# Hyena input weights: the low halves of a float32 split, by accumulating transfers instead of a GpSimd subtraction

## The chip, the cores and the metric

The kernel runs on one core of one Trainium2 chip. The metric is the device time of one execution in microseconds (us), the median over several runs. The engines of a core are TensorE (PE, with PEld for its weight loads), VectorE (DVE), ScalarE (ACT), GpSimd (POOL) and SyncE (SP), which work side by side and wait for each other by semaphores; a DMA is issued from the queue of SP, ACT or POOL and runs beside them.

## The reference, cut to what matters

The program is two small transformer blocks one after the other; the change lies in the last mixer, a Hyena layer over 512 tokens and 1024 channels:

```python
def hyena_mixer(h, w_in, conv_w, conv_b, f_w1, f_b1, f_w2, f_b2, f_w3, f_b3, freq, skip, w_out):
    L = h.shape[1]
    p = h @ w_in
    u = short_conv(p[..., :(HY_ORDER + 1) * HY_WIDTH], conv_w, conv_b)
    gate = p[..., (HY_ORDER + 1) * HY_WIDTH:]
    parts = jnp.split(u, HY_ORDER + 1, axis=-1)
    k_f = hyena_filters(L, f_w1, f_b1, f_w2, f_b2, f_w3, f_b3, freq)
    z = parts[0]
    for o in range(HY_ORDER):
        z = parts[o + 1] * long_conv(z, k_f[:, o], skip[o])
    return (z * jax.nn.silu(gate)) @ w_out
```

`h @ w_in` is a product of 512x1024 by 1024x4096, all in float32. `long_conv` is a convolution by Fourier transforms.

## The kernel before, in words

**The split product.** Each float32 operand is cut into a high part, rounded to the type float32r, and a low part that holds what the rounding lost. A block of the product is three float32r matmuls for each of 8 slices of the inner dimension: high by high, high by low of the data, and low of the weights by high (`mm3`, L192 to L194). The low part of a weight is `raw - high`.

**The weights.** `weight` prepares a tile of 1024x256 weights in two halves of 128 partitions by 1024 elements (512 KB). For each half SP issues the load into `wraw` (L177), ScalarE copies it to `wh` with rounding (L152, from `split`), and the subtraction `wl = wraw - wh` (L140) goes to the engine that the caller names. The tags `wraw`, `wh` and `wl` have two buffers each: two halves of raw weights, two whole tiles of high and of low parts. So a raw half is loaded again when the subtraction of the half before in its buffer has ended, and the next tile but one can be begun when TensorE has read the last of a tile's high part.

**The Hyena stage.** `hyena` takes 16 such tiles, in the order parts 0 and 1 for four channel groups, then parts 3 and 2; each tile serves two blocks of 128 channels (`block`), 48 matmuls in all, 24 to a block. Behind a block ScalarE and VectorE make the short convolution `v` out of the PSUM bank (L152, then two instructions of L143). Between blocks the generator `step` moves two `chain`s on, each of which takes a group of 128 channels through transposes, `spectrum` (matmuls, a ScalarE copy `spb`, VectorE sums `spt` and `X`), the product with the filter's spectrum `K` (`Y`, `pm`; one of the four products is GpSimd's), VectorE sums `spt` and `X` again, and the inverse transform (L1810, `obank`). `K` is loaded by a DMA from ScalarE's queue (L1782). A scheduler lays down one order of instructions for each engine before the run, and each engine keeps to its order: an instruction that waits holds up all behind it.

The low parts of these 16 tiles are made by GpSimd (`eng=nc.gpsimd`, L1888). GpSimd's other work in the stage is one `pm` product for each long convolution and the gate products `zt`.

Of the kernel before, what the change touches and what calls it, by code (L numbers as in the profile page):

```python
# [9 lines left out]
F32 = mybir.dt.float32  # L10
# [3 lines left out]
AF = mybir.ActivationFunctionType  # L14
ALU = mybir.AluOpType
# [3 lines left out]
P = 128  # L19
S = 512  # L20
D = 1024
# [29 lines left out]
class Kern:  # L51
# [117 lines left out]
    def weight(self, src, kb, gain=None, eng=None):  # L169
        hi, lo = self.hl(self.wp, "w", 2, [P, 8, self.wcols])  # L170
        src = src.rearrange("(k p) c -> p k c", p=P)
        cols = src.shape[-1]
        h = (kb + 1) // 2
        for s in (slice(0, h), slice(h, kb)):
            n = s.stop - s.start
            raw = self.t([P, 4, self.wcols], F32, "wraw", 2, self.wp)[:, :n, :cols]
            self.nc.sync.dma_start(raw, src[:, s, :])  # L177
            hs, ls = hi[:, s, :cols], lo[:, s, :cols]
            if gain is None:
                self.split(raw, hs, ls, eng)  # L180
            else:
                for k in range(n):
                    g = gain[:, s.start + k : s.start + k + 1]
                    self.act(hs[:, k], raw[:, k], AF.Copy, scale=g)
                    self.stt(ls[:, k], raw[:, k], g, hs[:, k].bitcast(F32), ALU.mult, ALU.subtract)
        return hi, lo

    def mm3(self, out, wh, wl, xs, first=True, last=True):
# [1630 lines left out]
    def hyena(self, xT):  # L1819
        nc, a = self.nc, self.a  # L1820
        w_in = a["hy_w_in_2"][0]
        cw = [self.prm[f"hcw{j}"] for j in range(3)]
        cb = self.prm["hcb"]
        with self.sbuf("hy") as hp:
            self.dft = hp.tile([P, 8, P], F32, name="dft")
            nc.scalar.dma_start(self.dft, a["hy_dft"])
            self.idft = hp.tile([P, 2, 4, P], F32, name="idft")
            nc.scalar.dma_start(self.idft, a["hy_idft"])

            sw = hp.tile([P, 4, 24], F32, name="hcs")  # L1830
            for j, t in enumerate(cw + [cb]):
                nc.vector.tensor_copy(sw[:, j, 0:8], t[:, 0:8])
                self.tt(sw[:, j, 8:24], t[:, 8:24], self.rn, ALU.mult)
            ada = self.prm["ada1x"]
            h = self.modulated(xT, self.r, ada)
            vs, zs = {}, {}

            def block(w, part, ch, j):
                ps = self.bank()
                self.proj(ps, w, slice(j * P, j * P + P), h)  # L1840
                i = part * 8 + 2 * ch + j
                v = self.t((P, S), F32, f"v{part}{j}", 2 if part < 2 else 1, hp)
                vs[part, ch, j] = v
                if part == 3:
                    self.act(v, ps, AF.Silu)
                else:
                    self.short_conv(ps, [sw[:, q, i : i + 1] for q in range(3)], sw[:, 3, i : i + 1], v)

            def chain(ch, j):
                us = []  # L1850
                for part in range(2):
                    ps = self.obank()
                    v = vs[part, ch, j].rearrange("p (s r) -> p r s", r=4)
                    for r in range(4):
                        self.transpose(ps[:, r * P : r * P + P], v[:, r])
                    u = self.t([P, 4, P], F32, f"u{part}", 2, hp)
                    self.act(u.rearrange("p r c -> p (r c)"), ps, AF.Copy)
                    us.append(u)
                yield
                y = yield from self.long_conv(hp, us[0], 2 * ch + j)  # L1860
                z = self.t([P, 4, P], F32, "z", 2, hp)
                self.tt(z.rearrange("p r c -> p (r c)"), y, us[1].rearrange("p r c -> p (r c)"), ALU.mult)
                yield
                y = yield from self.long_conv(hp, z, 8 + 2 * ch + j)
                yt = self.t([P, 4, P], F32, "yt", 2, hp)
                self.act(yt.rearrange("p r c -> p (r c)"), y, AF.Copy)
                yield
                ps = self.obank()
                for r in range(4):
                    self.transpose(ps[:, r * P : r * P + P], yt[:, r])  # L1870
                z = self.t((P, S), F32, "zt", 8, hp)
                self.act(z.rearrange("p (s r) -> p r s", r=4), ps.rearrange("p (r s) -> p r s", r=4), AF.Copy)
                zs[ch, j] = z

            waiting, live = [], []

            def step(n):
                for _ in range(n):
                    if waiting and len(live) < 2:
                        live.append(chain(*waiting.pop(0)))  # L1880
                    if live:
                        c = live.pop(0)
                        if next(c, self) is not self:
                            live.append(c)

            def group(parts, ch):
                for part in parts:
                    w = self.weight(w_in[:, part * D + ch * 256 : part * D + ch * 256 + 256], 8, eng=nc.gpsimd)  # L1888
                    for j in range(2):
                        block(w, part, ch, j)  # L1890
                        step(3)
                if 0 in parts:
                    waiting.extend([(ch, 0), (ch, 1)])
                else:
                    for j in range(2):
                        todo.append((ch, j))

            todo, hs = [], {}

            def finish():  # L1900
                while todo and todo[0] in zs:
                    ch, j = todo.pop(0)
                    z = zs[ch, j]
                    self.tt(z, z, vs[3, ch, j], ALU.mult, nc.gpsimd)
                    self.tt(z, z, vs[2, ch, j], ALU.mult)
                    hs[ch, j] = z

            for parts in ((0, 1), (3, 2)):
                for ch in range(4):
                    group(parts, ch)  # L1910
                    finish()
            while waiting or live:
                step(1)
            finish()
            return [self.ready(hs[k // 2, k % 2], None, self.hl(self.hp, "h", 8)) for k in range(8)]
# [161 lines left out]
```

## Time and profile before

| what | value |
|---|---|
| time, median of 3 runs | 2274.51 us (2272.2 to 2276.02) |
| time of the profiled execution | 2274.32 us |
| span of the profiled execution | 2272.6 us |
| Hyena stage with its input weights in use | about 1888 to 2206 us of the span |
| stretch of it with long convolutions | about 1932 to 2167 us |
| GpSimd subtractions of weights in the whole program | 40, of which 32 are those of the Hyena stage |
| mean granted clock of TensorE | 0.958 of full speed |

The profiled execution is as long as the median (2274.32 against 2274.51 us), and 1.7 us of it lie outside the span. The span counts from the first to the last instruction, so a microsecond taken out of the chain of waits in the Hyena stage is a microsecond of the metric. Busy times of engines overlap and say nothing alone on what a change is worth.

### The profile page before, as it was taken

Reading aid. Unit: us, or ns where it says so; the run is one execution under the profiler, and the core shown is the slowest. Engines: PE = TensorE matmul, PEld = TensorE weight load, DVE = VectorE, ACT = ScalarE, POOL = GpSimd, SP = SyncE. Lnnn points to the kernel's source line nnn. Section 1 sums busy time; section 2 is a strip of 40 time slices with the busy share of each in tenths; the row PEclk is TensorE's granted clock in tenths of the full one; section 3 lists DMA queues with packets and bytes.
Section 4 is the critical chain, followed back from the end, with each engine's and each line's share of the span. In section 5 each row is a group of like instructions: output and inputs, shape, how many; then the busy total and the mean of one; then the engine's idle time right before and its main releaser. Section 6 shows DMA issues by size and latency. Waiting matters only on the chain.

```text
span 2272.6 us, 30099 instructions
## 1 busy us (share of the span) xinstructions
PE 2093.7 (92%) x11860; PEld 1742.6 (77%) x11860; DVE 1485.5 (65%) x2348; ACT 987.7 (43%) x1498; POOL 532.8 (23%) x474
## 2 busy tenths in 40 slices
PE   6689999999999999988999999989898998888897
PEld 5478888788888797766788887888787876777776
DVE  8677864767665636664566575565588754988843
ACT  5544443333233446664343233434477753222232
POOL 4768631000000100001000000322244433324321
PEclk9889899999999999999999999989999999999899
DMA  5212152334542321111243553312100032222221
GB/s 163 69 59 71 62 201 92 120 101 132 167 130 83 103 75 41 54 55 47 88 144 107 171 161 97 114 46 75 29 1 1 19 112 71 81 91 85 64 74 56
DMA packets 194516, 199.38 MB, mean 88 GB/s; under 512 B 15059, under 2 KB 184550, under 8 KB 194311
## 3 DMA queue, kind: packets, MB, share of 16 engines
q1 hardware_dynamic: 179703, 183.11, 25.4%
q10 hardware_dynamic: 14672, 14.35, 2.1%
q8 instruction: 93, 1.52, 0.3%
q14 instruction: 48, 0.39, 0.1%
HBM read 182.75 MB, written 14.68 MB: 87 GB/s over the span
## 4 chain that ended last, share of the span: by engine, by line
PE 67%; DVE 17%; ACT 4%; issue 4%; DMA 3%; POOL 3%; SPq 0%; DVEq 0%; ACTq 0%; POOLq 0%
PE bank L194 16%; PE bank L192 16%; PE bank L193 16%; PE pair L982 2%; PE sc L1379 2%; DVE spt L140 2%; DVE X L140 2%; DVE Y L140 2%; DVE wl L140 1%; DMA adaraw<-in_ada_w_dram 1%; POOL tm L140 1%; ACT wh L152 1%; PE obank L1810 1%; DMA wraw<-in_ffn_w_up_dram 1%; PE bank L1724 1%
## 5 line engine op out<-in xcount | busy, mean ns | idle before, releaser
L192 PE MATMUL bank<-hh,wh 128*128 128x512 f32 x1472 | 592.5, 403 | 13.4 <-DVE v L143 7.5
L194 PE MATMUL bank<-hh,wl 128*128 128x512 f32 x1472 | 589.1, 400 | 10.9 <-DVE wl L140 10.9
L193 PE MATMUL bank<-hl,wh 128*128 128x512 f32 x1472 | 588.5, 400 | 0.4 <-DVE hl L143 0.4
L152 ACT ACTIVATE wh<-wraw 128x1024 fp32r<-128x1024 f32 (+2 forms) x260 | 245.2, 962 | 352.8 <-PE bank L193 199.2
L140 POOL TENSOR_TENSOR sqa<-sqa,sq 128x512 f32<-128x512 f32 x47 | 70.1, 1492 | 1174.8 <-ACT sq L152 1174.8
L192 PEld LDWEIGHTS bank<-hh,wh 128*128 128x128 f32 x1472 | 282.4, 192 | 76.4 <-issue 7.3
L194 PEld LDWEIGHTS bank<-hh,wl 128*128 128x128 f32 x1472 | 282.3, 192 | 76.1 <-DVE wl L140 15.6
L193 PEld LDWEIGHTS bank<-hl,wh 128*128 128x128 f32 x1472 | 282.4, 192 | 62.0 <-DVE hl L143 2.0
L140 DVE TENSOR_TENSOR wl<-wraw,wh 128x1024 fp32r<-128x1024 f32 (+2 forms) x220 | 245.0, 1130 | 110.3 <-ACT wh L152 109.0
L140 POOL TENSOR_TENSOR wl<-wraw,wh 128x1024 fp32r<-128x1024 f32 x40 | 102.1, 2571 | 174.3 <-ACT wh L152 174.2
L192 PE MATMUL bank<-ah,wh 128*128 128x512 f32 x352 | 138.0, 392 | 0.0
L194 PE MATMUL bank<-ah,wl 128*128 128x512 f32 x352 | 136.6, 390 | 0.5 <-DVE wl L140 0.5
L193 PE MATMUL bank<-al,wh 128*128 128x512 f32 x352 | 137.0, 389 | 0.0
L140 DVE TENSOR_TENSOR fg<-bank,rn 128x512 f32<-128x512 f32 x76 | 52.4, 690 | 103.0 <-PE bank L194 102.4
L140 POOL TENSOR_TENSOR sl<-sp,wh 128x768 fp32r<-128x768 f32 x32 | 60.4, 1888 | 106.1 <-ACT wh L152 70.9
L143 DVE SCALAR_TENSOR_TENSOR adaaccx<-adaraw,silc,adaaccx 128x256 f32<-128x256 f32 x168 | 81.0, 482 | 2.3
L194 PEld LDWEIGHTS bank<-ah,wl 128*128 128x128 f32 x352 | 66.1, 188 | 15.7 <-DVE wl L140 1.7
L192 PEld LDWEIGHTS bank<-ah,wh 128*128 128x128 f32 x352 | 66.1, 188 | 13.6 <-ACT wh L152 0.5
L193 PEld LDWEIGHTS bank<-al,wh 128*128 128x128 f32 x352 | 66.1, 188 | 13.5
L143 DVE SCALAR_TENSOR_TENSOR fy<-fg,prm,fy 128x511 f32<-128x511 f32 x88 | 65.9, 749 | 14.0 <-ACT fy L152 12.7
L140 POOL TENSOR_TENSOR fX<-spt 128x256 f32<-128x256 f32 x64 | 61.5, 985 | 48.2 <-DVE spt L140 44.7
L1810 PE MATMUL obank<-X,idft 128*128 128x128 f32 x256 | 42.8, 323 | 30.2 <-DVE X L140 27.7
(559 smaller groups left out, 4293.0 us busy)
## 6 DMA issues: line engine op xcount, KB each, us to landing
wraw<-in_ffn_w_up_dram SPq DMA_DIRECT2D x88, 512.0 KB
adaraw<-in_ada_w_dram SPq DMA_DIRECT2D x24, 1024.0 KB
wraw<-in_ffn_w_down_dram SPq DMA_DIRECT2D x48, 384.0 KB
wraw<-in_hy_w_in_dram SPq DMA_DIRECT2D x32, 512.0 KB
wraw<-in_attn_w_in_dram SPq DMA_DIRECT2D x18, 512.0 KB
kspec<-fX SPq DMA_DIRECT2D x16, 512.0 KB
wraw<-in_ssm_w_glu_dram SPq DMA_DIRECT2D x16, 512.0 KB
wraw<-in_kv_w_dram SPq DMA_DIRECT2D x16, 512.0 KB
```

The lines of the kernel that those rows point to most:

```text
L140: (eng or self.nc.vector).tensor_tensor(out=out, in0=a, in1=b, op=op)
L143: self.nc.vector.scalar_tensor_tensor(out=out, in0=a, scalar=s, in1=b, op0=op0, op1=op1)
L152: return self.nc.scalar.activation(out, a, func, bias=bias, scale=scale, **k)
L192: mm(out, wh[k], xh, start=first and k == 0, stop=False)
L193: mm(out, wh[k], xl, start=False, stop=False)
L194: mm(out, wl[k], xh, start=False, stop=last and k == n - 1)
L982: mm(z[:, h, c0 + qq - q0 : c0 + S - q0], lhs, t[:, h, cc : cc + n], start=False, stop=True, skip_group_check=True)
L1379: mm(s, l, m[:, c], start=i == 0 and k % 2 == 0, stop=True, skip_group_check=True)
L1724: nc.tensor.matmul(ps[:, r * P : r * P + P], hid[:, r * P : r * P + P], wpm[0][:, i, o], start=True, stop=True)
L1810: nc.tensor.matmul(ps[:, r * P : r * P + P], self.idft[:, j, r], Q[:, j, r], start=j == 0, stop=j == 1)
```

## The change

The 16 tiles of Hyena input weights get a function of their own. The load and the rounding copy to the high part stay. ScalarE then writes minus the high part into `wl`, and a DMA from GpSimd's queue adds the raw weights to it in place (`accum_op=ALU.add`). GpSimd computes nothing for these tiles any more. Buffers and their counts stay as they were, and a raw half is now free when the adding transfer has landed.

```diff
--- before.py
+++ after.py
@@ -183,6 +183,19 @@
                     g = gain[:, s.start + k : s.start + k + 1]
                     self.act(hs[:, k], raw[:, k], AF.Copy, scale=g)
                     self.stt(ls[:, k], raw[:, k], g, hs[:, k].bitcast(F32), ALU.mult, ALU.subtract)
+        return hi, lo
+
+    def weight_dma(self, src):
+
+
+        hi, lo = self.hl(self.wp, "w", 2, [P, 8, self.wcols])
+        src = src.rearrange("(k p) c -> p k c", p=P)
+        for s in (slice(0, 4), slice(4, 8)):
+            raw = self.t([P, 4, self.wcols], F32, "wraw", 2, self.wp)
+            self.nc.sync.dma_start(raw, src[:, s, :])
+            self.act(hi[:, s], raw, AF.Copy)
+            self.act(lo[:, s], hi[:, s].bitcast(F32), AF.Copy, scale=-1.0)
+            self.nc.gpsimd.dma_start(lo[:, s], raw, accum_op=ALU.add)
         return hi, lo
 
     def mm3(self, out, wh, wl, xs, first=True, last=True):
@@ -1885,7 +1898,7 @@
 
             def group(parts, ch):
                 for part in parts:
-                    w = self.weight(w_in[:, part * D + ch * 256 : part * D + ch * 256 + 256], 8, eng=nc.gpsimd)
+                    w = self.weight_dma(w_in[:, part * D + ch * 256 : part * D + ch * 256 + 256])
                     for j in range(2):
                         block(w, part, ch, j)
                         step(3)
```

All lines behind the new function have numbers 13 higher. VectorE's order does not change by a row, SP's order keeps its rows with other line numbers, and TensorE's differs in the place of one row. ScalarE gets 32 instructions more, GpSimd 32 transfers in place of 32 subtractions. Where they stand differs from place to place, as these three places show.

The first is GpSimd's order in the middle of the stage, before; the names with 16941 and 16790 are two tiles of weights, and each `pm` is the product of a long convolution.

```order
L140 TENSOR_TENSOR wl_16791<-wraw_16792,wh_16790 128x1024
L140 TENSOR_TENSOR pm_16604<-X_16544,K_16542 128x512
L140 TENSOR_TENSOR wl_16791<-wraw_16796,wh_16790 128x1024
L140 TENSOR_TENSOR pm_16691<-X_16621,K_16619 128x512
L140 TENSOR_TENSOR wl_16942<-wraw_16943,wh_16941 128x1024
L140 TENSOR_TENSOR wl_16942<-wraw_16947,wh_16941 128x1024
L140 TENSOR_TENSOR pm_16768<-X_16708,K_16706 128x512
```

And the same place of the changed kernel, where the same tiles bear the numbers 16804 and 16957:

```order
L140 TENSOR_TENSOR pm_16616<-X_16556,K_16554 128x512
L198 DMA wl_16805<-wraw_16806 128x1024
L198 DMA wl_16805<-wraw_16811 128x1024
L140 TENSOR_TENSOR pm_16705<-X_16633,K_16631 128x512
L198 DMA wl_16958<-wraw_16959 128x1024
L140 TENSOR_TENSOR pm_16782<-X_16722,K_16720 128x512
L198 DMA wl_16958<-wraw_16964 128x1024
```

The subtractions have become transfers, the first tile's first half stands behind a `pm` instead of ahead of it, and the second tile's second half likewise.

The second place is ScalarE's order at the same tile (16941), before:

```order
L152 ACTIVATE wh_16941<-wraw_16943 128x1024
L152 ACTIVATE v_2561_16752<-bank_16727,hcs 128x512
L152 ACTIVATE wh_16941<-wraw_16947 128x1024
L152 ACTIVATE yt_16765<-obank_16756 128x512
L152 ACTIVATE zt_16788<-obank_16783 128x4x128
```

And of the changed kernel:

```order
L152 ACTIVATE wh_16957<-wraw_16959 128x1024
L152 ACTIVATE v_2561_16766<-bank_16741,hcs 128x512
L152 ACTIVATE wl_16958<-wh_16957 128x1024
L152 ACTIVATE wh_16957<-wraw_16964 128x1024
L152 ACTIVATE yt_16779<-obank_16770 128x512
L152 ACTIVATE wl_16958<-wh_16957 128x1024
L152 ACTIVATE zt_16802<-obank_16797 128x4x128
```

Two instructions on a half of weights have come in, and what stands behind them (`yt`, `zt`) comes one or two places later.

The third is ScalarE's order at the last two tiles of the stage, where no chain stands between the blocks any more, before (17752 is the last tile but one, 17816 the last):

```order
L152 ACTIVATE wh_17752<-wraw_17758 128x1024
L152 ACTIVATE yt_17644<-obank_17635 128x512
L152 ACTIVATE v_2731_17671<-bank_17646 128x512
L152 ACTIVATE zt_17678<-obank_17673 128x4x128
L152 ACTIVATE v_2739_17715<-bank_17690,hcs 128x512
L152 ACTIVATE wh_17816<-wraw_17818 128x1024
L152 ACTIVATE v_2741_17744<-bank_17719,hcs 128x512
L152 ACTIVATE wh_17816<-wraw_17822 128x1024
```

And of the changed kernel (17780 and 17846):

```order
L152 ACTIVATE wh_17780<-wraw_17787 128x1024
L152 ACTIVATE yt_17670<-obank_17661 128x512
L152 ACTIVATE v_2731_17697<-bank_17672 128x512
L152 ACTIVATE wl_17781<-wh_17780 128x1024
L152 ACTIVATE zt_17704<-obank_17699 128x4x128
L152 ACTIVATE wl_17781<-wh_17780 128x1024
L152 ACTIVATE v_2739_17743<-bank_17718,hcs 128x512
L152 ACTIVATE wh_17846<-wraw_17848 128x1024
L152 ACTIVATE v_2741_17772<-bank_17747,hcs 128x512
L152 ACTIVATE wl_17847<-wh_17846 128x1024
L152 ACTIVATE wh_17846<-wraw_17853 128x1024
L152 ACTIVATE wl_17847<-wh_17846 128x1024
```

Here both negated copies of a tile stand behind a `v`, the second of tile 17780 behind a `zt` as well.

## Rows read from the trace of the kernel before

**Rows 1.** Page, part 1: busy time, share of span, instructions of each engine.

```profile
PE 2093.7 (92%) x11860; PEld 1742.6 (77%) x11860; DVE 1485.5 (65%) x2348; ACT 987.7 (43%) x1498; POOL 532.8 (23%) x474
```

**Rows 2.** Windows of the Hyena stage: stretch, length, busy PE, PEld, DVE, ACT, POOL.

```profile
1932.00:2167.00 235.00, 199.56 (x1087) 170.43 (x1086) 204.72 (x314) 63.95 (x87) 84.83 (x41) 0.93 0.25 77
2167.00:2206.00 39.00, 34.50 (x152) 27.64 (x150) 16.97 (x22) 16.81 (x23) 14.38 (x7) 1.00 0.28 87
```

**Rows 3.** Waits of PE, 1932 to 2167: total us, times, longest.

```profile
PE obank L1810 <- DVE X L140: 27.7, 9, 6.2
PE pair L1645 <- DVE z L140: 3.5, 1, 3.5
PE obank L1810 <- issue: 2.4, 1, 2.4
PE bank L192 <- DVE v L143: 1.7, 1, 1.7
```

**Rows 4.** Groups of DVE, 1932 to 2167: count, busy us, mean ns, idle before.

```profile
L140 DVE TENSOR_TENSOR X<-spt 128x256 f32<-128x256 f32 x128 | 62.8, 551 | 0.3
L140 DVE TENSOR_TENSOR Y<-X,K 128x512 f32<-128x512 f32 x32 | 34.2, 1104 | 0.2
L140 DVE TENSOR_TENSOR spt<-Y 128x512 f32<-128x512 f32 x32 | 27.0, 881 | 0.4
L140 DVE TENSOR_TENSOR Y<-Y,pm 128x512 f32<-128x512 f32 x32 | 24.1, 784 | 2.4 <-POOL pm L140 2.4
L143 DVE SCALAR_TENSOR_TENSOR v<-bank,hcs,v 128x511 f32<-128x511 f32 x30 | 22.3, 742 | 9.6 <-ACT v L152 9.5
```

**Rows 5.** DVE instructions on tile X, same stretch: minimum, median, maximum in ns.

```profile
L140 DVE TENSOR_TENSOR X<-spt x128: 409/419/2609, 1934.3 to 2164.8; 128x256 f32<-128x256 f32 x128
L140 DVE TENSOR_TENSOR Y<-X,K x32: 675/692/2879, 1935.8 to 2157.5; 128x512 f32<-128x512 f32 x32
```

**Rows 6.** Timeline of POOL: start, duration, line, instructions, idle before.

```profile
2071.29 5.05 POOL L140 TENSOR_TENSOR wl<-wraw,wh 128x1024 fp32r<-128x1024 f32 x2
...
2119.20 5.54 POOL L140 TENSOR_TENSOR wl<-wraw,wh 128x1024 fp32r<-128x1024 f32 x2
```

**Rows 7.** Timeline of DVE beside those two pairs of subtractions.

```profile
2070.16 6.79 DVE L140 TENSOR_TENSOR X<-spt 128x256 f32<-128x256 f32 x4
...
2118.08 4.46 DVE L140 TENSOR_TENSOR spt<-Y 128x512 f32<-128x512 f32 x2
2122.58 3.45 DVE L140 TENSOR_TENSOR X<-spt 128x256 f32<-128x256 f32 x4
```

**Rows 8.** Timeline of PE: what it waited for just behind them.

```profile
2077.01 3.36 PE L1810 MATMUL obank<-X,idft 128*128 128x128 f32 x14 [3.80 <-DVE X L140]
...
2125.17 0.77 PE L1810 MATMUL obank<-X,idft 128*128 128x128 f32 x2 [6.16 <-DVE X L140]
```

**Rows 9.** Group of POOL's weight subtractions, 1888 to 2206.

```profile
L140 POOL TENSOR_TENSOR wl<-wraw,wh 128x1024 fp32r<-128x1024 f32 x30 | 75.7, 2542 | 87.4 <-ACT wh L152 87.4
```

**Rows 10.** Waits of DVE for ACT, 1932 to 2167.

```profile
DVE spt L140 <- ACT spb L152: 12.5, 3, 6.7
DVE v L143 <- ACT v L152: 9.5, 5, 6.4
```

**Rows 11.** Timeline of ACT: issue of a K load; the last two tiles' high parts.

```profile
2022.95 0.33 ACTq L1782 DMA_DIRECT2D K<-kspec  x1
...
2165.52 2.01 ACT L152 ACTIVATE wh<-wraw 128x1024 fp32r<-128x1024 f32 x2 [4.90 <-PE bank L193]
...
2178.84 1.06 ACT L152 ACTIVATE wh<-wraw 128x1024 fp32r<-128x1024 f32 x1 [4.59 <-PE bank L193]
```

**Rows 12.** GB/s of the DMA engines in 40 slices, 2022.9 to 2026.2.

```profile
GB/s 0 0 0 0 0 0 0 0 0 0 0 0 248 149 149 149 50 149 199 99 348 149 199 99 248 348 397 348 447 496 348 447 496 298 249 248 0 0 0 0
```

**Rows 13.** Timeline of SP's queue: issue of a load of raw weights.

```profile
1890.35 0.37 SPq L177 DMA_DIRECT2D wraw<-in_hy_w_in_dram  x1
```

**Rows 14.** GB/s of the DMA engines in 40 slices, 1890.3 to 1898.

```profile
GB/s 0 0 0 0 0 37 170 133 181 255 314 383 383 378 282 160 48 59 192 122 160 234 314 378 378 378 282 192 37 0 0 0 0 0 0 0 0 0 0 0
```

## The prediction

> **What bounds the kernel now.** I begin with the page's busy times [rows 1]: TensorE 92%, GpSimd 23%. Read alone they say that work taken from GpSimd is worth nothing. That is an average over stages with different limits, so the next view is the windows of the one stage that the change touches [rows 2]. Between 1932 and 2167 us VectorE is busy 204.72 of 235 us, more than TensorE's 199.56; behind 2167, where the long convolutions are over, it is busy 16.97 of 39. So the first stretch is where VectorE can hold TensorE up. The view of TensorE's waits says that it does [rows 3]: all that TensorE waits for there is VectorE (or nothing that the trace shows), 27.7 + 3.5 + 2.4 + 1.7 = 35.3 us in 12 waits. That is the most that a faster VectorE can give back here.
>
> Is VectorE's work as long as it must be? The groups give means, the view of one tile gives the median [rows 4, 5]. 128 sums into X take 551 ns on the mean but 419 at the median; 32 products Y take 1104 against 692. The two other groups of the same 128x512 shape, 881 and 784 ns, I set against the same 690. So instructions of one shape differ widely, and the maxima (2609 and 2879 ns) say that a few are very long. The lost time is 128 x 0.132 + 32 x (0.412 + 0.191 + 0.094) = 16.9 + 22.3 = 39 us. The timelines say where the long ones lie: beside GpSimd's weight subtractions [rows 6, 7]. A pair of them from 2071.29 for 5.05 us stands beside four X that take 6.79 us; a pair from 2119.20 beside two spt that take 4.46 and four X that take 3.45. Elsewhere four X take 1.4 us by the median less the overlap of their ends, two spt 1.3. TensorE's wait comes right behind: 3.80 and 6.16 us for X [rows 8].
>
> The instruction of the same engine that reads its large operand from PSUM, v, takes 742 ns on the mean of 30 [rows 4], and the timeline gives no v another duration; it is the ones with two SBUF operands that stretch. That bears on what a transfer from GpSimd's queue will do. The Trainium skill, "SBUF — State Buffer", section "Who interferes with whom", says that a VectorE instruction with two SBUF inputs contends with a GpSimd instruction that reads SBUF, and not with one that only writes. The rows above agree with its first half. By its second half the issue of a transfer, which writes descriptors, would leave these sums alone, and the first rival below would give no other time than the forecast.
>
> **The change part by part.**
>
> *Subtractions removed.* 32 go, 30 of them inside 1888 to 2206, at 2542 ns each [rows 9]. GpSimd's own time is not on the path; what counts is the time that they take from VectorE. Of the 39 us above, the pm products, which stay and also run on GpSimd, cause part: in seven places of the VectorE timeline a pair of Y beside a pm takes about 1.0 us more than 1.3. Subtractions are left with 39 - 7 = 32 us, and a few single pm and zt instructions of VectorE beside them (about 3) make 35. I went through the stretch weight by weight: nine of the pairs stretch VectorE, and behind each stands a TensorE wait, or two. Taking each time the smaller of the two (3.80 of 5.4 behind the first pair of rows 6, 5.2 of 6.16 behind the second, and so on), the sum is 31 us. This is the gain if nothing else comes in: **-31**.
>
> *Negated copies added.* 32 ScalarE instructions of the size of the rounding copy, 1.06 us each [rows 11], 34 us in all, on an engine that is busy 63.95 of 235 us [rows 2]. What is queued behind them are v, spb, u, yt and zt of other blocks. The cover is that VectorE has other sums to do meanwhile; where it has none it waits for ScalarE: 8 times, 3 for spb and 5 for v [rows 10]. If each of these came 1.05 us later, it would cost 8.4 us; if VectorE's queue covers all, nothing. The order shows negated copies ahead of yt, zt or v in several places, so I take a little over half: **+5**. If the cover were gone everywhere in the stretch, it would be 22 copies x 1.05 = 23 us (a rival).
>
> *The transfer, and the loop of a raw buffer.* No accumulating transfer and no transfer from GpSimd's queue is in this trace, so its time from issue to landing, X, is bounded from both sides. The nearest row is a load of K, also 512 KB in rows of 4 KB: issued at 2022.95, its bytes move from 2023.9 to 2025.9 [rows 11, 12], that is 2.9 us with 2.0 of moving. Lower end: X = 2.9, a plain copy. Upper end: source read, destination read and destination write each take 2.0, and the issue takes GpSimd as long as the subtraction did: 0.9 + 6.0 + 2.5 = 9.4, say 9.5. I take X = 6: two reads of 2.0 with the write beside them, as the K load writes beside its read, the start of 0.9, and an issue of 1, an estimate between the 0.33 of ScalarE's queue and 2.5.
>
> Now the loop. A raw buffer is loaded (issue at 1890.35, first burst over at about 1893.6, 3.3 us [rows 13, 14]), read by the rounding copy (1.05), waits for a v between (0.77) and the negated copy (1.05), and is free when the transfer has landed: 6.2 + X, or 12.2 us. The 15 tiles behind the first take 318 us, 21 us each, and some 19 after the gain: fits. In the last two tiles and the first few, where blocks follow without chains, the distance is 2178.84 - 2165.52 = 13.3 us [rows 11]: fits by one microsecond. Above X = 7.1 each microsecond costs about four weights one each; at 9.5 that is 10 us. Within X = 6 I set **+2** for the places where a half now stands behind a pm in GpSimd's order.
>
> *SP and GpSimd's queues.* SP's loads now wait for the transfer's landing instead of the subtraction's end, which the loop holds already. On GpSimd, pm and zt stand behind a transfer's issue that waits for the negated copy; before they stood behind a subtraction that waited for the rounding copy and then ran 2.5 us. I cost this at nothing: the copy is 1.05 us later and the issue shorter by more than that. At an issue of 2.5 us it would be the 1.05 that pm comes later, which VectorE waited for 2.4 us in two places [rows 4].
>
> The sum is -31 + 5 + 2 = -24, from 2274.3 (the profiled execution, equal to the median): **2250 us**.
>
> **The rivals.**
>
> *The issue holds VectorE in the subtraction's place.* Speaks for it: GpSimd must read and write something to issue, and any GpSimd instruction beside two-operand sums has stretched them. Against: an issue moves no 512 KB. At an issue of 1 us that holds as the subtraction does, 1/2.54 of the 35 us stays, 14; the gain is 17 - 7 = 10: 2264. At 2.5 us per issue nothing is gained and the +7 remains: 2281. The Trainium skill, "SBUF — State Buffer", section "Summary: rules for kernel authors", speaks against the change in the other direction: a transfer from GpSimd's queue is starved while VectorE is in one of its faster modes. No group of VectorE in the stretch is of the operations that the page gives those modes (copy, cast, tensor_scalar), so by that page X would not grow here; no run here shows it yet.
>
> *ScalarE becomes the wait.* All 22 negated copies of the stretch (11 tiles by the timeline) come on the path: -31 + 23 + 2 = -6, 2268. For: ScalarE keeps its order and its copies wait for TensorE. Against: it is idle 171 of 235 us.
>
> *The loop becomes the bound, and the kernel slower.* From 6.2 + X = 21 on, X = 15, the stage is as long as today whatever VectorE does, and every further microsecond costs 15. At X = 17: 2274 + 30 = 2304. For: the buffer is held for a path through DMA that no row prices. Against: 15 us for 512 KB is five times the K load.
>
> **How the numbers follow.** Less than 0.2% (4.5 us) is no change that this kernel's times can tell. Forecast 0.62, its own range 2239 (all of the 35.3 us) to 2264 (X = 9.5, ScalarE at 8.4). Issue holds 0.14, half of it within no change or above. ScalarE 0.09. Loop 0.11. Two or three smaller losses together, in no case named, 0.04. Faster: 0.62 + 0.07 + 0.07 = 0.76. Same: 0.04 + 0.02 + 0.03 = 0.09. Slower: 0.15. The range runs from 2239, under which I see 0.04, to 2281, the upper end of the first rival, over which 0.13 are left.
>
> **What would show it.** Right: mean of X near 420 ns and of Y near 750, TensorE's waits for X under 10 us in the stretch, VectorE busy some 170 us. The transfer: the wait of SP's loads for it, and TensorE's waits for wl in the last two tiles, none at X = 6. ScalarE: VectorE's waits for spb and v, under 30 us in total. Wrong: long X beside the issues on GpSimd (first rival); VectorE waiting for ScalarE much longer (second); wh waiting for the load of wraw in every tile (third).

## The result, and the profile after

The changed kernel takes 2243.76 us (median of four runs, 2240.12 to 2255.53) against 2273.36 for the kernel before (four runs): a ratio of 0.988, 95% interval 0.9839 to 0.9922, so about 27 to 30 us are gained (the interval allows 18 to 37). The profiled execution took 2240.97 us.

Its span is 2239.2 us against 2272.6, 33.4 less. Of this, 3.6 us lie ahead of the first instruction that the change adds: the last two matmuls `stat<-epsd,ones` ahead of the stage start at 1841.13 us in the trace of before and at 1837.49 in the trace of after. This point lies anywhere between 1833.3 and 1848.2 in the twelve profiled executions of this document, so single spans are compared from there on: 431.5 us before, 401.7 after, 29.8 less, as between the medians (29.6).

The page's busy times answer to [rows 1]. GpSimd lost 53 us and ScalarE gained 29; TensorE lost 13 us of busy time with the same number of matmuls, and VectorE lost 31 with the same number of instructions.

```profile
PE 2080.3 (93%) x11860; PEld 1730.8 (77%) x11860; DVE 1454.8 (65%) x2348; ACT 1016.7 (45%) x1530; POOL 480.3 (21%) x474
```

**The whole stage.** I take the windows from the first matmul of the Hyena product to the first of the product behind it: stretch, length, busy PE, PEld, DVE, ACT, POOL, granted clock, share and rate of DMA. The kernel before:

```profile
1898.00:2206.64 308.64, 267.36 (x1378) 224.52 (x1379) 238.93 (x361) 94.14 (x127) 108.73 (x52) 0.94 0.25 77
```

The kernel after:

```profile
1899.35:2173.66 274.31, 257.59 (x1379) 215.98 (x1379) 208.65 (x361) 121.46 (x155) 62.00 (x52) 0.97 0.58 144
```

The stage is 34.3 us shorter, and the two rows split that. TensorE's time outside its matmuls fell from 308.64 - 267.36 = 41.3 us to 274.31 - 257.59 = 16.7: 24.6 us. Its matmuls, as many as before (one more record in the second trace), take 9.8 us less, and the granted clock is 0.97 in place of 0.94. VectorE's work, also as much as before, takes 30.3 us less.

**TensorE's waits** in 1932 to 2135, the convolutions' stretch, in the columns of [rows 3]:

```profile
PE obank L1823 <- DVE X L140: 8.4, 8, 2.0
PE pair L1658 <- DVE z L140: 1.6, 1, 1.6
PE obank L1823 <- issue: 0.9, 1, 0.9
```

35.3 us became 10.9, and no wait is longer than 2.0 us where 6.2 stood.

**VectorE's groups** in that stretch answer to [rows 4], and the view of tile X to [rows 5]:

```profile
L140 DVE TENSOR_TENSOR X<-spt 128x256 f32<-128x256 f32 x128 | 46.6, 423 | 0.3
L140 DVE TENSOR_TENSOR Y<-X,K 128x512 f32<-128x512 f32 x32 | 32.2, 1041 | 0.2
L143 DVE SCALAR_TENSOR_TENSOR v<-bank,hcs,v 128x511 f32<-128x511 f32 x32 | 23.7, 741 | 10.4 <-ACT v L152 10.3
L140 DVE TENSOR_TENSOR spt<-Y 128x512 f32<-128x512 f32 x32 | 22.8, 750 | 0.5
L140 DVE TENSOR_TENSOR Y<-Y,pm 128x512 f32<-128x512 f32 x32 | 21.8, 713 | 2.4 <-POOL pm L140 2.4
```

```profile
L140 DVE TENSOR_TENSOR X<-spt x128: 406/415/1385, 1936.7 to 2130.3; 128x256 f32<-128x256 f32 x128
```

X has its median as its mean (423 against 415), and v, which reads PSUM, is where it was. Y is not: 1041 ns. The timelines of GpSimd and VectorE at one place show both cases side by side (start, duration, line, instructions):

```profile
1945.03 0.87 POOL L198 DMA_DIRECT2D wl<-wraw  x1 [5.07 <-ACT wl L152]
...
1948.99 1.29 POOL L140 TENSOR_TENSOR pm<-X,K 128x512 f32<-128x512 f32 x1 [1.06 <-DVE X L140]
```

```profile
1945.22 1.09 DVE L140 TENSOR_TENSOR X<-spt 128x256 f32<-128x256 f32 x3
...
1949.36 2.07 DVE L140 TENSOR_TENSOR Y<-X,K 128x512 f32<-128x512 f32 x2
```

Three X beside a transfer's issue of 0.87 us take 1.09 us, which is unstretched. Two Y beside a pm of 1.29 us take 2.07 in place of 1.28. In the whole stretch 12 of 16 pairs of Y lie beside a pm and are 0.7 to 1.5 us too long, 11.6 us together: that is most of what is left of VectorE's lost time, and the change does not touch it. In two of the other four pairs the pm beside them takes 3.4 us and the two Y 1.28: there GpSimd's product is the long one.

The same can be counted for the whole stage. I take what each VectorE instruction lasts above the median of its group, and put it down to the GpSimd instruction that overlaps it longest. Before, 31.3 us stand beside subtractions, 9.0 beside pm and 4.9 beside the gate products zt; after, 0.0 beside the transfers' issues (53 instructions), 11.3 beside pm and 4.4 beside zt.

**VectorE's waits for ScalarE**, to hold against [rows 10]:

```profile
DVE spt L140 <- ACT spb L152: 10.8, 3, 5.1
DVE v L143 <- ACT v L152: 10.3, 3, 6.4
```

22.0 us became 21.1, with 32 more copies on ScalarE.

**The transfer itself**, in the page's part on DMA issues (count, size, median from issue to landing):

```profile
wl<-wraw POOLq DMA_DIRECT2D x32, 512.0 KB, 5.6
```

**A loss at the head of the stage.** The chain that ended last runs, ahead of the first Hyena matmul, through one of the first transfers (start, duration, engine):

```profile
1875.95 0.83 POOL wl L198
1876.78 6.82 DMA wl<-wraw
1883.66 4.28 DMA wraw<-in_hy_w_in_dram
...
1888.92 0.62 ACT sq L152
1889.59 3.58 PE stat L288 x16
```

A transfer holds a raw buffer, the load of the next half waits for it, ScalarE's wh waits for the load, and a square (sq) for the norm ahead of the stage stands behind that wh on ScalarE. ScalarE's timeline, before:

```profile
1875.68 2.01 ACT L152 ACTIVATE wh<-wraw 128x1024 fp32r<-128x1024 f32 x2 [3.86 <-PE bank L193]
...
1886.84 2.00 ACT L152 ACTIVATE wh<-wraw 128x1024 fp32r<-128x1024 f32 x2 [3.86 <-PE bank L193]
1888.75 0.61 ACT L152 ACTIVATE sq<-xT 128x512 f32<-128x512 f32 x1
```

And after:

```profile
1872.04 2.01 ACT L152 ACTIVATE wh<-wraw 128x1024 fp32r<-128x1024 f32 x2 [3.86 <-PE bank L206]
...
1885.39 1.06 ACT L152 ACTIVATE wh<-wraw 128x1024 fp32r<-128x1024 f32 x1 [6.06 <-DMA wraw<-in_hy_w_in_dram]
1887.96 1.06 ACT L152 ACTIVATE wh<-wraw 128x1024 fp32r<-128x1024 f32 x1 [1.51 <-DMA wraw<-in_hy_w_in_dram]
1888.92 0.61 ACT L152 ACTIVATE sq<-xT 128x512 f32<-128x512 f32 x1
```

From one pair of rounding copies to the next it took 1886.84 - 1875.68 = 11.2 us; now the first copy comes 13.4 us behind and the second, counted from the end of the first of that pair (1873.05), 14.9. TensorE's timeline before, and after:

```profile
1889.41 1.05 PE L275 MATMUL stat<-ones,sq 128*128 128x1 f32 x8 [2.38 <-ACT sq L152]
```

```profile
1889.59 1.86 PE L288 MATMUL stat<-ones,sq 128*128 128x1 f32 x8 [6.19 <-ACT sq L152]
1891.31 1.84 PE L288 MATMUL stat<-ones,sqa 128*128 128x1 f32 x8
```

TensorE waits 3.8 us longer, and the 8 small matmuls behind the wait take 1.86 us instead of 1.05: the granted clock of these matmuls' window is 0.50 (1.2 GHz) against 0.81 before, behind a pause of 6.19 us instead of 2.38. From the start of these matmuls to the first Hyena matmul it is 9.76 us against 8.59. So about 3.8 + 1.2 = 5 us are lost here. From the last `stat<-epsd,ones` to the first Hyena matmul, which I call the head, it is 61.9 us against 56.9. With the stage's 34.3 us this gives the whole: -34.3 + 5.0 - 0.4 (behind the stage) = -29.7, which but for rounding is the 29.8 above.

### The profile page after: what moved, and what is told of

Its sections match the earlier page's. It is cut to its first block, busy times and chain, and to the rows that moved or that the text cites. A ratio compares the mean times of both kernels' runs of the same rounds, so it can differ in the third digit from the quotient of the medians.

```text
span 2239.2 us, 30162 instructions
## 1 busy us (share of the span) xinstructions
PE 2080.3 (93%) x11860; PEld 1730.8 (77%) x11860; DVE 1454.8 (65%) x2348; ACT 1016.7 (45%) x1530; POOL 480.3 (21%) x474
## 4 chain that ended last, share of the span: by engine, by line
PE 63%; DVE 18%; POOL 5%; ACT 5%; DMA 4%; issue 4%; SPq 0%; DVEq 0%; POOLq 0%; ACTq 0%
PE bank L205 15%; PE bank L207 15%; PE bank L206 15%; PE pair L995 2%; PE sc L1392 2%; DVE spt L140 2%; POOL tm L140 2%; DVE Y L140 2%; DVE wl L140 2%; DMA adaraw<-in_ada_w_dram 2%; DVE X L140 1%; ACT wh L152 1%; DMA wraw<-in_ffn_w_up_dram 1%; DVE adaaccx L143 1%; PE pair L969 1%
## 5 line engine op out<-in xcount | busy, mean ns | idle before, releaser
L205 PE MATMUL bank<-hh,wh 128*128 128x512 f32 x1472 | 589.7, 401 | 13.3 <-DVE v L143 5.8
L207 PE MATMUL bank<-hh,wl 128*128 128x512 f32 x1472 | 586.7, 399 | 12.3 <-DVE wl L140 12.2
L206 PEld LDWEIGHTS bank<-hl,wh 128*128 128x128 f32 x1472 | 280.6, 191 | 61.9 <-DVE hl L143 2.2
L140 POOL TENSOR_TENSOR sl<-sp,wh 128x768 fp32r<-128x768 f32 x32 | 60.4, 1888 | 98.6 <-ACT wh L152 68.4
L205 PEld LDWEIGHTS bank<-ah,wh 128*128 128x128 f32 x352 | 66.1, 188 | 13.3
L143 DVE SCALAR_TENSOR_TENSOR fy<-fg,prm,fy 128x511 f32<-128x511 f32 x88 | 65.8, 748 | 13.9 <-ACT fy L152 12.7
L152 ACT ACTIVATE sq<-xT 128x512 f32<-128x512 f32 x49 | 30.6, 626 | 83.9 <-DVE xT L140 60.9
L152 ACT ACTIVATE fy<-fg,prm 128x512 f32<-128x512 f32 x44 | 35.6, 809 | 66.5 <-DVE fg L140 66.5
```

The lines of the kernel that those rows point to most:

```text
L140: (eng or self.nc.vector).tensor_tensor(out=out, in0=a, in1=b, op=op)
L143: self.nc.vector.scalar_tensor_tensor(out=out, in0=a, scalar=s, in1=b, op0=op0, op1=op1)
L152: return self.nc.scalar.activation(out, a, func, bias=bias, scale=scale, **k)
L205: mm(out, wh[k], xh, start=first and k == 0, stop=False)
L206: mm(out, wh[k], xl, start=False, stop=False)
L207: mm(out, wl[k], xh, start=False, stop=last and k == n - 1)
```

## The experiments

My theory: GpSimd's subtractions stretch VectorE's sums because they read SBUF at the same time; the changed kernel gains what that cost, and gives a few microseconds back at the head through the raw buffer's loop. Rivals: GpSimd's queue, being shorter, is what counts; or the transfers do (their DMA traffic, or ScalarE's extra copies). Ratios are to the kernel before, run on the same chip, with 95% intervals.

**The change again**, as the base of the next three.

> The changed kernel itself, timed again so that the next three have a base on the same chip. Expected by all theories: 0.984 to 0.992 of the kernel before, about 2244 us. In the trace: VectorE's X near 420 ns on the mean, TensorE's waits for VectorE near 11 us in the stretch with long convolutions.

Measured: 2244.38 us, 0.987 [0.9846, 0.9894]. The first stat matmul waits 6.1 us again, and the stage takes 274.29 us in its trace against 274.31 in the first: the stage repeats far more closely than the whole time, and the table at the end of this section gives it for every run.

**The subtraction back on GpSimd**, its result read by nobody, beside the transfers; in 28 of the 32 halves (not in the first two tiles), 960 of 1024 columns, in two instructions. The main lines of the edit:

```diff
-            self.act(lo[:, s], hi[:, s].bitcast(F32), AF.Copy, scale=-1.0)
+            neg = self.act(lo[:, s], hi[:, s].bitcast(F32), AF.Copy, scale=-1.0)
+            if busy is not None:
+                for i in (0, 480):
+                    self.tt(busy, raw.rearrange("p k c -> p (k c)")[:, i : i + 480], hi[:, s].rearrange("p k c -> p (k c)")[:, i : i + 480].bitcast(F32), ALU.subtract, self.nc.gpsimd)
             self.nc.gpsimd.dma_start(lo[:, s], raw, accum_op=ALU.add)
```

> The changed kernel with GpSimd computing raw minus high again for 14 of the 16 tiles, into a scratch tile that nobody reads (960 of 1024 columns of a half, in two instructions of 128x480); the transfers stay. Theory 'ports' (the gain is that VectorE's two-operand instructions are no longer held up by GpSimd instructions that read SBUF): X goes back to about 550 ns and the time to 2268 to 2278 us. Theory 'order' (the gain comes from the other order of ScalarE and GpSimd, or from the clock): the time stays within 5 us of 2244.

Measured: 2283.48 us, 1.0045 [1.0026, 1.0064]. The group on GpSimd in the stage, then X on VectorE and TensorE's wait for X from 1932 to 2165:

```profile
L140 POOL TENSOR_TENSOR junk<-wraw,wh 128x480 f32<-128x480 f32 x56 | 80.3, 1434 | 84.2 <-ACT wh L152 81.2 <-POOL pm L140 0.9 <-issue 0.7
```

```profile
L140 DVE TENSOR_TENSOR X<-spt 128x256 f32<-128x256 f32 x124 | 58.7, 531 | 0.2
```

```profile
PE obank L1826 <- DVE X L140: 27.3, 11, 3.8
```

Everything that the change took away is back: X at 531 ns (551 before), 27.3 us of waits (27.7 before). Against the change it costs (1.0045 - 0.987) x 2272.8 = 40 us, with an uncertainty of 7 from the two intervals; the stage alone is 36.6 us longer. It comes out above the kernel before and above my range of 2268 to 2278: the stage is 2.3 us longer than before, and the loss at the head is still there too (63.4 us against 56.9).

**One operand only**, in the same 28 halves: GpSimd copies the high part, 128x480 twice per half, instead of subtracting (`gpsimd.tensor_copy(busy, hi[...])` in the place of `self.tt`).

> As the kernel with the subtraction back, but GpSimd copies the high half into the scratch tile (two copies of 128x480, one operand read, one written). Theory 'ports': a GpSimd instruction that reads SBUF holds VectorE as long as it lasts; if a copy takes GpSimd half of the subtraction's 2.5 us a half, about half of the loss, 2254 to 2262 us. Theory 'GpSimd's queue' (pm and zt come earlier because GpSimd is free): the loss goes by GpSimd's busy time alone, with VectorE's durations as short as in the changed kernel.

Measured: 2252.78 us, 0.991 [0.9887, 0.9934]: 9 us above the change, with an uncertainty of 8, a little under my range of 2254 to 2262; the stage is 9.7 us longer. I had expected half of the subtractions' loss for half of their time; it is a quarter of the loss for more than half of the time (44.5 of 80.3 us), and why a copy costs so much less is not shown. GpSimd's group, and X:

```profile
L200 POOL COPY junk<-wh 128x480 f32<-128x480 f32 x56 | 44.5, 794 | 81.6 <-ACT wh L152 80.4
```

```profile
L140 DVE TENSOR_TENSOR X<-spt 128x256 f32<-128x256 f32 x128 | 51.8, 463 | 0.3
```

**Write only**: four memsets of 128x480 for each of these halves, behind a one-column copy by ScalarE that ties them to the half; some of them stand behind the transfers in GpSimd's order, not ahead of them. The main lines:

```diff
+            if busy is not None:
+                self.act(busy[:, 0:1], hi[:, s][:, 0, 0:1].bitcast(F32), AF.Copy)
+                for i in range(4):
+                    self.nc.gpsimd.memset(busy, 0.0)
```

> As the kernel with the subtraction back, but GpSimd only writes: four memsets of 128x480 into the scratch tile for each half, tied to the half by a one-column ScalarE copy of about 0.2 us. Theory 'ports': VectorE's durations stay short (X under 440 ns), the time within 6 us of 2244. Theory 'GpSimd's queue': a loss in proportion to the memsets' busy time, as in the copy kernel.

Measured: 2243.81 us, 0.9873 [0.9845, 0.9901], the time of the change. GpSimd's group, and X:

```profile
L201 POOL MEMSET junk<- 128x480 f32 x112 | 64.2, 573 | 15.8 <-ACT junk L152 12.0
```

```profile
L140 DVE TENSOR_TENSOR X<-spt 128x256 f32<-128x256 f32 x128 | 46.7, 425 | 0.3
```

This is the run that tells the theories apart. GpSimd is busy for 64.2 us with memsets and nothing is lost (the stage takes 274.27 us); it was busy for 44.5 us with copies and 9 us were lost, for 80.3 with two-operand subtractions and 40 us. Nor did the memsets miss VectorE's work: counted as above, 100 of VectorE's instructions lie beside memsets and are 0.2 us too long together, 53 beside the copies 9.4 us, 63 beside the subtractions 28.2 us. What GpSimd reads counts, not how long it is occupied. The Trainium skill, "SBUF — State Buffer", section "Who interferes with whom", says that GpSimd instructions that only write do not contend with VectorE's two-input instructions and that reading ones do; the three runs agree, with the numbers above.

**The first two tiles subtracted as before**, the other 14 by transfers:

```diff
-                    w = self.weight_dma(w_in[:, part * D + ch * 256 : part * D + ch * 256 + 256])
+                    cols = w_in[:, part * D + ch * 256 : part * D + ch * 256 + 256]
+                    w = self.weight(cols, 8, eng=nc.gpsimd) if 0 in parts and ch == 0 else self.weight_dma(cols)
```

> The changed kernel, but the first two tiles (parts 0 and 1 of the first channel group), which are prepared while the stage before still runs, are made by GpSimd's subtraction as before. Theory 'loop at the head' (in the changed kernel ScalarE's last square before the norm stands behind a rounding copy whose raw half waits for the first tile's transfer, 6.8 us, and then for its load, 4.3 us): TensorE's wait for that square falls from 6.2 to about 2.4 us and the time by 4 to 6 us, to 2238 to 2240. Rival 'nothing lost there': 2244 within 2 us.

Measured: 2234.01 us, 0.9834 [0.9815, 0.9853]. TensorE's wait at the head, in the view of its waits from 1880 to 1900, is back at the value of before:

```profile
PE stat L288 <- ACT sq L152: 2.4, 1, 2.4
```

Against the change's 0.987 this is (0.987 - 0.9834) x 2272 = 8 us, with an uncertainty of 7 from the two intervals. The traces give 6.3 and 8.4 us against the two of the change, from the point ahead of the stage on: 5.0 and 7.0 at the head, 1.0 in the stage, 0.4 behind it. It beats both kernels.

**The raw weights added from HBM** instead of from the raw buffer, so that no transfer holds the buffer:

```diff
-            self.nc.gpsimd.dma_start(lo[:, s], raw, accum_op=ALU.add)
+            self.nc.gpsimd.dma_start(lo[:, s], src[:, s, :], accum_op=ALU.add)
```

> The adding transfer reads the weights from HBM a second time instead of from the raw half in SBUF, so that a raw half is free when the rounding copy has read it; 16 MB more are read from HBM. Theory 'loop' (load, copies and transfer share one buffer): the waits of ScalarE's rounding copies for loads go (11 us in the changed kernel's stage), the wait at the head too; 2236 to 2241 us. Rival 'transfer on the path' (wl itself is late): rows of 1 KB in place of 4 KB make the transfer longer, TensorE waits for wl, 2244 to 2255.

Measured: 2237.63 us, 0.9854 [0.9839, 0.9868]. The wait for sq is 2.4 us here too, though each transfer takes longer:

```profile
wl<-in_hy_w_in_dram POOLq DMA_DIRECT2D x32, 512.0 KB, 8.1
```

So the head's loss is the loop of the buffer and not the transfer's length by itself. The intervals do not settle whether this kernel is better than the change; its trace does: a head of 56.5 us and a stage of 272.9, 6.8 us less than the change in the two together.

**Without the adding transfers** (the line above deleted).

> Leaves out the adding transfers: wl stays minus the high part. What is left of the change's price is ScalarE's negated copies. Theory 'loop': as with the add from HBM, 2236 to 2241 us, since with the raw buffer free early nothing else of the transfer is on the path. Rival 'the transfer costs elsewhere' (GpSimd's issues of 0.86 us, DMA traffic): below 2233.

Measured: 2234.8 us, 0.9837 [0.9819, 0.9855]; the wait for sq is 2.4 us. The time lies between my two ranges (2236 to 2241, and below 2233), and the interval of about 4 us covers both. The traces decide: without the transfers the stage is 0.3 us shorter than with the adding from HBM, so neither their issues nor their DMA traffic cost more than that in the stage.

**Without any low part** (no negated copies, no transfers; `return hi, hi`).

> Leaves out the low parts of these tiles altogether: the third matmul reads the high part again, so TensorE's work is the same and nothing is made for wl, neither on ScalarE nor on GpSimd nor by DMA. This is the floor for any way of making them. Theory 'ScalarE costs about 5 us' (the prediction's second term): 5 us below the kernel without the add, 2231 to 2236. Rival 'covered': within 2 us of it.

Measured: 2233.9 us, 0.9836 [0.9815, 0.9857]. That is the floor: what the stage costs when the low parts cost nothing. The two last runs differ by the 32 negated copies and by nothing in time that their intervals can tell (0 ± 6 us), as the rival 'covered' had it; in their traces the stage is 1.9 us shorter without the copies. The kernel with the first two tiles subtracted is on the same floor within the intervals.

**Each transfer made twice** (the `dma_start` line doubled).

> The changed kernel with every adding transfer made twice, the second behind the first (wl then holds the low part plus the raw weights, so the output is another). This doubles the time that a raw half is held by transfers, from about 5.6 to about 11 us, and adds one issue on GpSimd for each half. Theory 'loop': at the head the square before the norm comes 5 to 7 us later, and in the first and last tiles, where tiles follow at about 12 us, the loop of 6.2 + 11 = 17 us is the bound, three to four times 4 us; in the middle (18 us a tile) hardly anything: 2260 to 2272 us. Rival 'covered': 2244 to 2250.

Measured: 2280.2 us, 1.0033 [1.0015, 1.0051], 37 us above the change: more than I expected. The page's row, ScalarE's wait for raw weights from 1932 to 2165, and TensorE's waits from 1880 to 2210:

```profile
wl<-wraw POOLq DMA_DIRECT2D x64, 512.0 KB, 5.4
```

```profile
ACT wh L152 <- DMA wraw<-in_hy_w_in_dram: 42.2, 12, 11.6
```

```profile
PE obank L1824 <- DVE X L140: 21.2, 11, 4.9
PE bank L208 <- DMA wl<-wraw: 8.5, 3, 7.8
PE bank L206 <- ACT hh L152: 5.8, 1, 5.8
PE pair L1659 <- ACT u L152: 4.0, 1, 4.0
PE obank L216 <- ACT yt L152: 3.8, 2, 3.6
```

X itself is short (425 ns on the mean, as in the change), so the 21.2 us are not VectorE's sums but what comes late to them. I had counted only on tiles that follow each other closely. A wh that waits up to 11.6 us for its load holds ScalarE, which keeps its order, and behind it stand u and yt that the convolutions need in the middle of the stage, and spb and v: VectorE waits 19.2 us for spb and 26.9 for v from 1932 to 2165, where it was 10.8 and 10.3 in the change's stretch. GpSimd adds a little: a pm now also stands behind a second transfer that waits for the first, and VectorE waits 6.1 us for pm, 2.4 in the change.

At the head my expectation failed the other way. In this run's order the square stands ahead of the waiting wh; TensorE waits 1.6 us for it, and then 5.8 in place of 2.2 for hh, which stands behind that wh. The head takes 59.2 us, 2.3 more than before and less than with single transfers. What the loop costs at the head hangs on what the scheduler puts behind the waiting copy.

**VectorE makes the subtractions**, no transfers (the kernel before without `eng=nc.gpsimd`).

> The kernel before with the subtraction of these 32 halves on VectorE (1.13 us each by its other subtractions of the size) instead of GpSimd. No transfer, no negated copy. Theory 'ports': VectorE's sums are short again (X near 420 ns) but it has 22 x 1.13 = 25 us more of its own in the stretch, against some 30 us of stretched sums before: TensorE's waits for VectorE 25 to 35 us, the time 2262 to 2272 us, not more than 10 below the kernel before. Rival 'GpSimd's latency' (2.5 us a half instead of 1.13 is what hurt): 2245 to 2252.

Measured: 2249.21 us, 0.9899 [0.9876, 0.9922]: better than I expected, 15 us above the floor (12 in the stage). The groups of VectorE from 1932 to 2150:

```profile
L140 DVE TENSOR_TENSOR X<-spt 128x256 f32<-128x256 f32 x128 | 45.5, 415 | 0.0
...
L140 DVE TENSOR_TENSOR wl<-wraw,wh 128x1024 fp32r<-128x1024 f32 x23 | 27.9, 1215 | 11.1 <-ACT wh L152 11.0
```

23 subtractions put 27.9 us on the engine that I called the bound, and in the whole only 15 came out: VectorE's idle time took the rest. In the whole stage VectorE is busy for 32.9 us more than in the kernel without low parts, and idle for 44.2 us in place of 65.5.

The time falls into the range of the rival, that the 2.5 us of a subtraction on GpSimd is what hurt, by making wl late. The rival's reason is not the one: in the kernel before TensorE waits for no wl in the whole stage, and in the run with the subtraction back the loss came with a result that nobody reads. What my own range had wrong is that it put all of VectorE's added work on the path. So even VectorE doing the work itself is cheaper than GpSimd doing it beside VectorE, by (1 - 0.9899) x 2272 = 23 us.

**The stage and the head of every run**, from the traces of one execution each, in us. The stage and its columns are as in the two rows of the whole stage above; "outside" is the stage less TensorE's matmuls; the head runs from the last `stat<-epsd,ones` to the first Hyena matmul, and two traces of the one changed kernel differ by 2 us in it.

| run | stage | matmuls | outside | granted clock | VectorE busy | head |
|---|---|---|---|---|---|---|
| before | 308.6 | 267.4 | 41.3 | 0.94 | 238.9 | 56.9 |
| the change | 274.3 | 257.6 | 16.7 | 0.97 | 208.7 | 61.9 |
| the change again | 274.3 | 257.6 | 16.7 | 0.97 | 208.8 | 63.9 |
| subtraction back | 310.9 | 269.9 | 41.0 | 0.93 | 237.0 | 63.4 |
| one operand only | 284.0 | 259.3 | 24.7 | 0.97 | 218.8 | 61.5 |
| write only | 274.3 | 257.8 | 16.5 | 0.97 | 208.8 | 61.5 |
| first two tiles subtracted | 273.3 | 256.6 | 16.7 | 0.97 | 208.4 | 56.9 |
| added from HBM | 272.9 | 255.4 | 17.5 | 0.98 | 210.2 | 56.5 |
| no adding transfers | 272.6 | 256.3 | 16.3 | 0.98 | 208.4 | 56.4 |
| no low part | 270.7 | 257.0 | 13.7 | 0.98 | 205.2 | 58.5 |
| each transfer twice | 313.8 | 269.4 | 44.5 | 0.93 | 208.5 | 59.2 |
| VectorE subtracts | 282.3 | 259.0 | 23.4 | 0.97 | 238.1 | 56.4 |

In these rows the clock goes with TensorE's waits and not with what causes them. With each transfer twice VectorE's sums are short, and TensorE, waiting for late data, is granted 0.93 as with the subtractions:

```profile
1898.46:2212.28 313.82, 269.35 (x1378) 224.74 (x1379) 208.46 (x359) 122.62 (x155) 85.58 (x83) 0.93 0.78 177
```

## Why the prediction was right, and where its terms were off

2250 us was forecast, 2243.8 came. The forecast's mechanism holds, but its terms were mis-sized, and the errors partly cancel: that the sum came within 6 us is in this part luck, the direction and the cause are not.

*VectorE no longer stretched, -31.* The step was right in kind: taking GpSimd's reads away and putting them back moved the waits out and in again. VectorE's work shrank by 30.3 us where I had 35 to give back: only 31.3 stood beside subtractions, and pm and zt, for which I had taken off 7, cost 13.9 us before and 15.7 after. So Y stayed at 1041 ns, and the sign "Y near 750" was wrong. TensorE's time outside its matmuls gave back 24.6 us, not 31. What I left out, when I called 35.3 us the most that a faster VectorE can give back, is that TensorE, waiting less, was granted a higher clock: 9.8 us less for the same matmuls. Together 34.4, near 31 by two errors against each other. The table bears this out: with the waits put back, by subtractions or by late transfers, the clock is at 0.93 again and the matmuls are as long as before. What else the clock answers to was not tried. The runs give the gain without the loss at the head as 0.0166 x 2271.5 = 38 us (first two tiles subtracted).

*ScalarE's copies, +5.* Two at most: without and with the copies the ratio is 0.9836 and 0.9837 (0 ± 6 us), the stage is 1.9 us longer with them in the traces, and VectorE's waits for ScalarE did not grow. The upper bound of 8.4 and the rival of 23 us both fall; nearly all of the copies lie in ScalarE's idle time.

*The loop of the raw buffer, +2.* X was 5.6 us (6 taken) and an issue 0.87 (1 taken), but the term was too small, because I took the distance of the last two tiles, 13.3 us, for the first few too. The rows of before show 11.2 there, and a loop of 12.2 or more does not fit into that. The second half comes 14.9 us behind; two transfers, issued within 1.9 us, are under way there. The step "SP and GpSimd's queues, costed at nothing" also failed at this place: it looked only at what stands behind the issue on GpSimd, not at ScalarE's square behind the waiting wh. Measured: 5 us at the head, and 8 ± 7 between the medians, of which the traces place 1.0 in the stage. In the last two tiles the loop did fit: TensorE waits for no wl there.

*The rivals.* The issue does not hold VectorE: the 53 instructions beside an issue are unstretched. ScalarE is not the wait. The loop as the bound needed X = 15 by my working; two transfers of 5.4 us in a row were already enough to be slower than before, so this rival was nearer than I had it, because ScalarE's order spreads the delay over the stage.

## What to carry to other kernels

Look for instructions of one shape whose mean is far above their median, and lay the other engines' timelines beside the long ones: here the subtractions of a GpSimd that was busy 23% cost 38 us through reads that stretch VectorE. When a buffer is held longer, compare its new loop with the shortest distance between two uses everywhere, the entry to the stage included, and ask what stands behind the instruction that waits, on an engine that keeps its order. A transfer that does arithmetic is worth using only while its loop fits; where it doesn't (here two tiles of 16), the old way is the better one, or a source that does not hold the buffer: adding from HBM has the longer transfers and, by its trace, the shorter time.

## What the runs showed of the hardware

- GpSimd's effect on VectorE's two-operand sums goes by what it reads: 64.2 us of memsets cost nothing, 44.5 us of one-operand copies 9 us, 80.3 us of two-operand subtractions 40 us. Beside them VectorE's instructions are 0.2, 9.4 and 28.2 us too long.
- The one that takes longer can also be GpSimd's: two of its 128x512 products last 3.4 us in place of 1.29, with the two VectorE products beside them as short as alone (1.28 us).
- An accumulating transfer of 512 KB from SBUF to SBUF lands 5.6 us after its issue, and 8.1 us with the source in HBM; the issue occupies GpSimd for 0.87 us and leaves VectorE alone.
- TensorE's matmuls got 9.8 us shorter in a stage of 308.64 us in which only its waits were cut, the granted clock rising from 0.94 to 0.97. With the waits put back, by GpSimd's reads or by late transfers, they take 269.9 and 269.4 us at 0.93.
